# Marking every DMA of a batched matrix product as a single packet

## The chip, the cores and the metric

The kernel runs on one core of a Trainium2 chip. The time is the device time of one execution in microseconds. Every execution quoted with an interval was of the fast state; kernels with a single timing are of unknown state and are said to be single. A profile's span is some 2 us shorter than the device time (121.4 against 123.31 us for the kernel before); it runs from the start of the first instruction in the trace to the end of the last. Ratios are the mean time of one kernel's fast runs over the mean of the other's of the same rounds, so they are not quite the ratios of the medians quoted beside them.

## The reference

```python
batch, m, k, n = 16, 512, 512, 512
a: (batch, k, m) float32,  b: (batch, k, n) float32
return np.matmul(a.transpose(0, 2, 1), b).astype(np.float32)
```

The kernel reads 2 x 16.8 MB and writes 16.8 MB. Both inputs are cast to bfloat16 on the way to the matrix engine.

## The kernel before

Two batches ("a pair") stand in a tile of 128 partitions, 64 each. A partition holds 8 rows of 512 floats, which lie side by side in memory: one run of 16 KB. (With a size, a run is here such a stretch of bytes.) The first loads and the two halves of the last one have 4 rows, 8 KB. A store moves 8 KB from each partition for each batch. SP issues all 24 DMAs, on one queue. The profile lists 16 DMA engines. Shared evenly among them (an estimate: the trace's 1664 rows of 16 KB over 13 loads and 16 engines are 8 each), an engine moves 8 partitions of each DMA: 8 runs of a load, 32 runs of a store of four batches.

```python
in_v = [x.rearrange("(pair g) (q r) m -> pair (g q) r m", g=G, r=R) for x in (a, b)]
out_v = out.rearrange("batch (c t) n -> c batch t n", t=T)
# ...
for n in range(2, 2 * pairs):
    if n >= NX:                                  # NX = 4 input buffers
        nc.sync.wait_ge(s_in, n - NX + 1)        # free when DVE has cast the buffer
    src, x = in_v[n % 2][n // 2], x_ts[n % NX]
    if n < 2 * pairs - 1:
        nc.sync.dma_start(x[:], src).then_inc(s_x[n % NX], 16)
    # ... (the last load in two halves)
nc.sync.wait_ge(s_h, 16)                         # stores only after the loads
for i in range(0, NO, 2):
    n = min(2, NO - i)
    nc.sync.wait_ge(s_out, i + n)
    nc.sync.dma_start(out_v[:, G * i:G * (i + n)],
        o_t[:, i:i + n].rearrange("p i g t n -> p (i g) t n")).then_inc(s_o if i else s_o0, 16)
# ... casts on DVE, matmuls on PE, copies of PSUM on ACT
nc.sync.dma_start(out_v[:, batch - G:batch], o_ts[(pairs - 1) % NO])   # the last store
```

## Time and profile before

| | kernel before |
|---|---|
| device time, median | 123.31 us (123.14 to 123.31, 3 runs) |
| span of the profile | 121.4 us |
| PE, DVE, ACT busy | 51%, 31%, 27% |
| sixteen DMA engines | 97.7% |
| 2 MB load, issue to landing | 12.2 us (a), 15.9 us (b) |

A DMA is said to land with the last of its sixteen semaphore writes (the trace has 384 of them, records of 4 B, for 24 DMAs). The table reads as follows. A compute engine that is busy half of the time has room; the DMA engines have none. So the time is the number of bytes over the rate at which the engines move them (50.33 MB at the load window's 429 GB/s are 117.3 us), plus the two ends. The lines that carry this are shown in the prediction.

### The profile page before, as it was taken

How to read it: one execution, taken by the hardware profiler on the slowest of the kernel's cores; microseconds unless marked ns; L12 is line 12 of the kernel's file. 1: busy time of each engine (PE TensorE's matmuls, PEld its weight loads, DVE VectorE, ACT ScalarE, POOL GpSimd, SP SyncE). 2: the span in 40 equal slices, each digit the busy share in tenths (PEclk: the TensorE clock that was granted, in tenths of full speed). 3: DMA queues.
4: the chain of work that ended last, by engine and by line, in shares of the span. 5: the costliest groups of instructions: out<-in, count | busy, mean ns of one | idle time of the engine just before them, and what ended most of it. 6: DMA issues, size and time to landing. Idle time of an engine off the chain costs nothing.

```text
span 121.4 us, 1204 instructions
## 1 busy us (share of the span) xinstructions
PE 61.7 (51%) x480; PEld 35.0 (29%) x480; DVE 38.1 (31%) x48; ACT 32.2 (27%) x41; POOL 0.2 (0%) x4
## 2 busy tenths in 40 slices
PE   0007829099379559959919979989800000000000
PEld 0002314066156225536515636655400000000000
DVE  0061160864284090484265347492000000000000
ACT  4000423302900920390560084190009200000000
POOL 0000000000000000000000000000000000000000
PEclk9999999999999967999995999999995555555555
DMA  2999999999999999999999999999999999999994
GB/s 57 424 432 429 467 432 432 432 432 432 432 432 432 432 432 427 432 432 416 432 427 427 432 432 402 432 427 427 429 429 432 429 429 432 421 424 429 429 424 208
DMA packets 4864, 50.33 MB, mean 415 GB/s; under 512 B 384, under 2 KB 384, under 8 KB 384
## 3 DMA queue, kind: packets, MB, share of 16 engines
q1 hardware_dynamic: 4864, 50.33, 97.7%
HBM read 33.55 MB, written 16.78 MB: 415 GB/s over the span
## 4 chain that ended last, share of the span: by engine, by line
DMA 63%; DVE 6%; issue 3%; ACT 2%; SPq 2%; ACTq 1%
DMA x<-in_b_dram 53%; DMA out_dram<-o 10%; DVE bbf L118 3%; DVE abf L118 3%; ACT o L181 2%; SPq L74 1%; ACTq L70 1%; SPq L72 1%; SPq L80 0%; DVE done L124 0%; ACT done L186 0%; SPq L219 0%; SPq L70 0%
## 5 line engine op out<-in xcount | busy, mean ns | idle before, releaser
L156 PE MATMUL ps<-bbf,abf 64*128 64x512 bf16 x448 | 53.0, 393 | 13.6 <-PEq L151 13.6
L156 PEld LDWEIGHTS ps<-bbf,abf 64*128 64x128 bf16 x448 | 31.3, 112 | 35.3 <-issue 20.6
L181 ACT COPY o<-ps 128x1024 f32<-128x1024 f32 x28 | 26.3, 1026 | 45.9 <-PE ps L156 37.0
L118 DVE CAST abf<-x 128x2048 bf16<-128x2048 f32 x14 | 17.1, 1224 | 17.5 <-PE ps L156 13.5
L118 DVE CAST bbf<-x 128x2048 bf16<-128x2048 f32 x14 | 17.1, 1225 | 14.6 <-DMA x<-in_b_dram 14.6
L136 PE MATMUL ps<-bbf,abf 128*128 128x512 bf16 x32 | 8.7, 433 | 12.4 <-PEq L134 12.4
L136 PEld LDWEIGHTS ps<-bbf,abf 128*128 128x128 bf16 x32 | 3.7, 121 | 16.9 <-issue 14.8
L175 ACT COPY o<-ps 128x1024 f32<-128x1024 f32 x4 | 4.0, 1012 | 15.9 <-PE ps L136 15.9
L99 DVE CAST abf<-x 128x2048 bf16<-128x2048 f32 x2 | 2.5, 1228 | 11.2 <-DMA x<-in_a_dram 5.8
L99 DVE CAST bbf<-x 128x2048 bf16<-128x2048 f32 x2 | 2.5, 1225 | 1.2 <-DMA x<-in_b_dram 1.2
L186 ACT ACTIVATE done<-done 1x1 uint32<-1x1 uint32 x8 | 1.6, 197 | 0.0
L175 ACT ACT_TABLE_LOAD x1 | 1.3, 1283 | 0.9 <-SPq L70 0.9
L124 DVE MEMSET done<- 1x1 f32 x14 | 0.8, 59 | 0.0
L103 DVE MEMSET done<- 1x1 f32 x2 | 0.1, 59 | 0.0
L208 POOL MEMSET const-bfloat16-1.0<- 128x1 bf16 x1 | 0.1, 102 | 0.0
L208 POOL MEMSET const-uint8-127<- 128x1 uint8 x1 | 0.1, 102 | 0.0
L208 POOL MEMSET const-float32-0.0<- 128x1 f32 x1 | 0.1, 99 | 0.2 <-issue 0.2
L208 POOL MEMSET const-float32-1.0<- 128x1 f32 x1 | 0.1, 99 | 0.0
## 6 DMA issues: line engine op xcount, KB each, us to landing
x<-in_a_dram SPq DMA_DIRECT2D x7, 2048.0 KB, 12.2
x<-in_b_dram SPq DMA_DIRECT2D x6, 2048.0 KB, 15.9
out_dram<-o SPq DMA_DIRECT2D x3, 4096.0 KB, 21.7
x<-in_b_dram SPq DMA_DIRECT2D x4, 1024.0 KB, 12.1
out_dram<-o SPq DMA_DIRECT2D x2, 2048.0 KB, 29.3
x<-in_a_dram SPq DMA_DIRECT2D x2, 1024.0 KB, 6.8
```

Source lines behind the costliest of these rows:

```text
L70: with tc.tile_critical(no_gpsimd_drain=True):
L72: nc.sync.dma_start(x_ts[j][:, 0:RV, :], in0_v[j][0]).then_inc(s_f[j], 16)
L74: nc.sync.dma_start(x_ts[j][:, RV:R, :], in0_v[j][1]).then_inc(s_x[j], 16)
L99: nc.vector.tensor_copy(out=bf_ts[0][:], in_=x_ts[j][:, u * RV:(u + 1) * RV, :]).then_inc(s_cast, 1)
L118: nc.vector.tensor_copy(out=(bbf_ts if n % 2 else abf_ts)[v][:], in_=x_ts[n % NX][:, v * RV:(v + 1) * RV, :],).then_inc(s_cast, 1)
L124: nc.vector.memset(dve_done[:, n:n + 1], 0.0).then_inc(s_in, 1)
L136: mm = nc.tensor.matmul(ps_ts[0][h][:, t % 2, :], a_m[:, r, t], bbf_ts[0][:, r, :], start=(r == 0), stop=(r == RV - 1),)
L156: mm = nc.tensor.matmul(ps_ts[g][h][:, t % 2, :], a_m[:, t], bbf_ts[v][rows, r, :], start=(v == 0 and r == 0), stop=(v == V - 1 and r == R ...
L175: nc.scalar.copy(out=o_ts[0][:, g, 2 * h:2 * h + 2, :], in_=ps_ts[0][h][:]).then_inc(s_ev[h], 1)
L181: ev = nc.scalar.copy(out=o_ts[i % NO][:, g, 2 * h:2 * h + 2, :], in_=ps_ts[g][h][:])
L186: nc.scalar.memzero(act_done[:, i:i + 1]).then_inc(s_out, 1)
L208: nc = _bacc.Bacc("TRN2", target_bir_lowering=False, num_devices=1)
```

## The change

By its name, the flag `single_packet` asks that all runs which one DMA engine moves for a DMA form one packet. That reading is mine. In the kernel before, the trace has a record for each run (4480 data records for 4480 runs). The intent is to save whatever a packet costs at its boundary.

```diff
+    def dma(dst, src):
+        return nc.sync.dma_start(dst, src, single_packet=True)
...
-                nc.sync.dma_start(x[:], src).then_inc(s_x[n % NX], 16)
+                dma(x[:], src).then_inc(s_x[n % NX], 16)
...  (likewise the first loads, the last load's halves and all stores)
```

## The prediction

> **What bounds the kernel now.** I read the page first, at its busy table and its slices, then the DMA queue and the sizes of its packets, then the chain that ended last, and last the windows and the waits of the DMA queue's own engine.
>
> The page of the kernel before:
>
> ```profile
> PE 61.7 (51%) x480; PEld 35.0 (29%) x480; DVE 38.1 (31%) x48; ACT 32.2 (27%) x41; POOL 0.2 (0%) x4
> ...
> DMA  2999999999999999999999999999999999999994
> GB/s 57 424 432 429 467 432 432 432 432 432 432 432 432 432 432 427 432 432 416 432 427 427 432 432 402 432 427 427 429 429 432 429 429 432 421 424 429 429 424 208
> DMA packets 4864, 50.33 MB, mean 415 GB/s; under 512 B 384, under 2 KB 384, under 8 KB 384
> ...
> q1 hardware_dynamic: 4864, 50.33, 97.7%
> ...
> DMA 63%; DVE 6%; issue 3%; ACT 2%; SPq 2%; ACTq 1%
> ```
>
> No compute engine is busy much over half of the span, while the DMA row is at 9 (90% or more) in 38 of 40 slices, and the one data queue fills 97.7% of sixteen engines' time. The GB/s row is flat: there is no stage in which the DMA engines starve. So the kernel is bound by the DMA engines from 2 to 120 us, and the chain (63% DMA) says the same in another way. A compute saving would buy nothing; only a change of the time per byte, or of the two ends, can move the total.
>
> The windows, whose last two columns are the share of the DMA engines and their rate, put numbers on the stages (first loads in 8 KB rows, loads in 16 KB rows, stores in 8 KB rows):
>
> ```profile
> 2.00:12.70 10.70, 2.99 (x8) 1.09 (x9) 2.45 (x2) 0.18 (x1) 0.00 (x0) 1.00 1.01 413
> 12.70:76.00 63.30, 47.34 (x374) 27.13 (x374) 30.79 (x40) 23.24 (x30) 0.00 (x0) 0.95 1.00 429
> ...
> 80.80:120.10 39.30, 6.87 (x64) 4.04 (x59) 1.72 (x4) 5.23 (x8) 0.00 (x0) 0.63 1.00 424
> ```
>
> The reader is to see that the share stays at 1.00 in the load stage and in the store stage, with the store stage about 1% slower.
>
> The waits of the issuing engine, SP, tell whether the queue ever runs dry:
>
> ```profile
> SPq L80 <- DVE done L124: 43.8, 9, 8.3
> SPq L219 <- DMA out_dram<-o: 24.9, 1, 24.9
> ...
> x<-in_b_dram SPq DMA_DIRECT2D x6, 2048.0 KB, 15.9
> out_dram<-o SPq DMA_DIRECT2D x3, 4096.0 KB, 21.7
> ```
>
> SP waits for free buffers, but a 2 MB load takes 15.9 us from issue to landing, and at 432 GB/s its own transfer is 2.097 MB / 432 = 4.9 us. So some three loads stand in the queue at any time, and what it costs to issue or to start one is hidden behind the others. At the end SP waits 24.9 us for the last store: the tail is pure queue, too.
>
> **What the trace's DMA records add.** Taken one by one, the records of the data queue are of three sizes: 1664 of 16384 B that take 611 ns each, 2816 of 8192 B that take 309 ns, and 384 of 4 B that take 9 ns. The first two are the contiguous rows, one per partition (8 rows of 512 floats on a load; 4 rows on the first loads, on the last load's halves and on the stores); 384 = 24 DMAs x 16 engines are the semaphore writes. Per engine: 104 x 0.611 = 63.5, 176 x 0.309 = 54.4 and 24 x 0.009 = 0.2, together **118.1 us**; the first record starts at 1.97 us and the last ends at 120.07 us, which is also 118.1 us. The records tile the time of each engine without a hole. And two 8 KB records take 618 ns where one 16 KB record takes 611: so a record costs **7 ns plus 302 ns for each 8 KB**. The 7 ns is the only thing per run that a coarser packet could remove. 302 ns for 8192 B on 16 engines is 434 GB/s.
>
> [...]
>
> **The change part by part.** The order of instructions on each engine, compared between the two programs, is unchanged: 24 DMAs on SP, same shapes, same waits; the diff only adds a flag.
> - Removed: packet boundaries between the rows of one DMA on one engine. There are 104 + 176 = 280 data rows per engine in 24 DMAs, so 280 - 24 = 256 boundaries go. If the whole 7 ns is paid per packet, that is 256 x 7 = 1.79 us. [...] If the 7 ns belongs to the descriptor, it is 0. All of it lies on the path that sets the end, since the engines are never idle: whatever goes there shows in full.
> - Added: at most 0.4 us at the first load, where nothing hides it. [...] The semaphore writes remain: 24 per engine, 0.2 us.
> - Moved: the landing of each load, and with it DVE's casts, PE and the buffers' release, come earlier or later with the stream; PE has 49% of the span free, so it stays hidden. ACT's 8.9 us wait for the first store ends with that store; the last store is issued at 95.0 us, while its records begin only at 115.2, so there are 20 us of slack.
>
> The sum with a weight of 0.5 on the full 7 ns, 0.3 on half of it, 0.2 on nothing: 0.9 + 0.27 = 1.17 us off, minus some 0.1 for the start: about **1.1 us off 123.31, so 122.2 us**.
>
> **The rivals.**
> - *Nothing happens.* The 7 ns belong to each descriptor [...], or the records keep 611 and 309 ns: 123.3 us. [...] Against it: a fixed cost of 7 ns a record is plainly there.
> - *The long packet hurts.* An engine might [...] make a bubble at each of the 24 boundaries [...]. For it: [...] one store issue of SP took 5.5 us against 0.69 in the median[...]. [...] A bubble of 0.1 us at each of 24 boundaries gives +2.4 us, 124.6 us after the gain; one of 0.2 us gives over 126.
> - *The bound moves elsewhere.* With DMA 1.5% faster, would PE or DVE take over? PE 61.7 and DVE 38.1 us of 121.4 say no.
>
> **Range and chances.** The best case is 123.31 - 1.79 = 121.5 us, 1.5% off: even the full sum does not reach 2%. So faster by over 2% (under 120.8 us) would need a saving that I cannot see: 0.05. Slower by over 2% (over 125.8 us) is the second rival with bubbles of 0.17 us or more: 0.10. Within 2%: 0.85. The range of 8 in 10 runs from 121.3 (the best case with a little of the launch's spread, 0.17 us in the three runs) to 124.0 us (no gain and a small bubble).
>
> **What would show each step right or wrong.** Right: the number of DMA records falls from 4864 towards 24 x 16 of data plus 384, or it stays while a row takes 302 to 306 ns in place of 309 and 604 to 608 in place of 611; GB/s in load slices goes from 432 to 433 or 434, and the store window from 424 to 428 or more; the span goes down by 1 us or so with the DMA share still near 97.7%. Wrong towards the first rival: 611 and 309 unchanged. Wrong towards the second: zeros or sevens in the DMA row where there are nines, a GB/s row that dips at DMA boundaries, or records longer than 309 ns in the store stage. The start: the first landing, now at 5.8 us, should not come over 0.4 us later. [...]

Passages that rest on nothing these traces show are cut from the prediction, and the cuts are marked. The forecast's sum: 0.5 x 1.79 + 0.3 x 0.90 + 0.2 x 0 = 1.17 us off, and 1.1 us off after 0.1 us for the start. The 0.90 us is half of the 1.79 us, and that half of the 7 ns might be saved was not shown. The 0 to 0.4 us at the start was an estimate from the first issue, which took 0.39 us in the trace. "Descriptor" stands for a single run, whether it is joined with others or not.

## The result, and the profile after

The changed kernel took 123.17 us in the median (123.11 to 123.35, 4 runs) against 123.25 us of the kernel before in the same rounds (123.14 to 123.31). The ratio is 0.9997, with a 95% interval of 0.998 to 1.0014: no change. All outputs are right.

The page of the kernel after, its DMA rows, the count of packets and the data queue:

```profile
DMA  2999999999999999999999999999999999999994
GB/s 54 426 426 431 474 431 431 431 431 431 431 431 431 431 431 431 431 431 431 431 431 431 431 431 388 428 431 423 428 423 426 431 428 431 431 423 431 426 428 175
DMA packets 4864, 50.33 MB, mean 414 GB/s; under 512 B 384, under 2 KB 384, under 8 KB 384
...
q1 hardware_dynamic: 4864, 50.33, 97.6%
```

The count is the first thing to see: 4864 packets, as before. (What the page counts as packets are the records of the trace: each has a start, a length and a size.) If runs had been joined, and a record stood for a packet, 4480 data records would have become 384. The DMA row and the share (97.6% and 97.7%) are the same. The rates are the same too, which the windows show (columns: window and its length, busy time of PE, its weight load, DVE, ACT and POOL, the granted clock, the share of the DMA engines, GB/s). The kernel after:

```profile
12.70:76.00 63.30, 49.00 (x364) 26.97 (x364) 30.79 (x40) 23.24 (x30) 0.00 (x0) 0.93 1.00 430
...
80.80:120.10 39.30, 8.21 (x74) 4.75 (x70) 2.37 (x4) 6.92 (x10) 0.00 (x0) 0.67 1.00 425
```

Before, these two windows had 429 and 424 GB/s. Record by record, all 1664 rows of 16 KB take 611 ns in both traces, and of the 2816 rows of 8 KB all but some sixty take 309 ns in both. In steady state two 2 MB loads land 4862 ns apart in both traces, in the mean of twelve. Small differences elsewhere, such as PE's 64.9 us busy after against 61.7 before, lie on engines with idle time: the change did not touch their instructions, and PE's granted clock dips at other moments (its mean in the load window is 0.95 before and 0.93 after).

So nothing happened, to the nanosecond of a record. That is more than "the saving was small": even a flag that made one boundary cheaper by 1 ns would have moved the landings of 2 MB loads, with their 7 inner boundaries on each engine, by 7 ns. The question became whether the flag acts at all.

**What the built programs say.** Both kernels were compiled and the results compared. In the program handed to the compiler all 24 DMAs carry the flag, false before and true after. In the output, the instruction streams of all five engines are byte for byte the same; only the tables that map instructions to source lines differ, beside logs and the compiler's copy of its input. No run's page shows this; flag_off below has these same streams too. So the theory that I took to the chip: **the compiler drops the flag, and the chip runs the same program twice.** The rival: the flag acts by some other way, and does nothing visible at rows of 8 and 16 KB, where a boundary weighs little (by my reading, 7 of 309 and of 611 ns).

### The profile page after: what moved, and what is told of

The parts are those of the page before. It is cut to its first block, busy times and chain, and to the rows that moved or that the text cites. A ratio compares the mean times of both kernels' runs of the same rounds, so it can differ in the third digit from the quotient of the medians.

```text
span 121.6 us, 1204 instructions
## 1 busy us (share of the span) xinstructions
PE 64.9 (53%) x480; PEld 35.7 (29%) x480; DVE 38.0 (31%) x48; ACT 32.2 (26%) x41; POOL 0.2 (0%) x4
## 2 busy tenths in 40 slices
DMA packets 4864, 50.33 MB, mean 414 GB/s; under 512 B 384, under 2 KB 384, under 8 KB 384
## 3 DMA queue, kind: packets, MB, share of 16 engines
q1 hardware_dynamic: 4864, 50.33, 97.6%
HBM read 33.55 MB, written 16.78 MB: 414 GB/s over the span
## 4 chain that ended last, share of the span: by engine, by line
DMA 45%; DVE 7%; PE 4%; issue 3%; ACT 2%; ACTq 1%
DMA x<-in_b_dram 35%; DMA out_dram<-o 10%; PE ps L140 4%; DVE abf L122 4%; DVE bbf L122 3%; ACT o L185 2%; ACTq L74 1%; DVE done L128 0%; ACT done L190 0%
## 5 line engine op out<-in xcount | busy, mean ns | idle before, releaser
L140 PE MATMUL ps<-bbf,abf 128*128 128x512 bf16 x32 | 11.8, 552 | 12.5 <-PEq L138 12.5
L140 PEld LDWEIGHTS ps<-bbf,abf 128*128 128x128 bf16 x32 | 4.3, 139 | 19.6 <-issue 19.0
```

The source lines that it names most:

```text
L140: mm = nc.tensor.matmul(ps_ts[0][h][:, t % 2, :], a_m[:, r, t], bbf_ts[0][:, r, :], start=(r == 0), stop=(r == RV - 1),)
```

## The experiments

**The same program twice, and the noise.** flag_off is the changed kernel with

```diff
-        return nc.sync.dma_start(dst, src, single_packet=True)
+        return nc.sync.dma_start(dst, src, single_packet=False)
```

and flag_on is the changed kernel again, both five rounds on one chip.

> The changed kernel with the flag set to False: the kernel before under another name, for the noise of the method. Every theory: ratio 1.000 to the kernel before, with an interval of about 0.2% to each side.

> The changed kernel again, on the same chip as flag_off. Theory (the compiled instruction streams of the two programs came out byte for byte the same, so the flag does nothing on the chip): ratio 1.000, as flag_off within 0.1%, rows of 611 and 309 ns as before. Rival (the flag acts, and a small gain hides in the noise of the first four runs): 0.2 to 0.5 us under flag_off, or some rows under 611 ns.

| | median us | ratio to before | 95% interval |
|---|---|---|---|
| flag_off | 123.09 | 0.9992 | 0.9978 to 1.0006 |
| flag_on | 123.20 | 0.9997 | 0.9983 to 1.001 |

The kernel before under another name differs from itself by 0.08%, and the flag from that by 0.05%, in the wrong direction for a saving. A gain of 1.1 us would be 0.9%, far outside either interval. flag_on's rival (a gain of 0.2 us or more, hidden in noise) has no support left: flag_on came out 0.11 us above flag_off.

**Short runs, where a packet's cost would weigh.** The loads are cut into runs of 2 KB, without and with the flag; data and buffers stay the same, and the stores keep their 8 KB:

```diff
+    def load(dst, src):
+        return nc.sync.dma_start(dst, src, single_packet=False, max_dma_last_dim=2048)
...
-                dma(x[:], src).then_inc(s_x[n % NX], 16)
+                load(x[:], src).then_inc(s_x[n % NX], 16)
```

> Loads cut into runs of 2 KB (64 runs per engine for 2 MB), flag off. Theory (7 ns of fixed cost per run, on the path): a record of 2048 B takes 302/4 + 7 = 82 to 83 ns; per engine 1024 x 82.5 = 84.5 us of loads in place of 78.4, so 6 us more: 129.3 us. If the 7 ns is not a cost per run (but grows with the bytes): 77 ns and 123.3 us.

> As rows2k_off, with the flag on. Theory (the flag is dropped): 129.3 us and records of 82 to 83 ns, ratio to rows2k_off 1.000. Rival (the flag acts, but buys nothing at rows of 8 KB and more): the packets are joined, records of 76 to 79 ns, 122 to 126 us, 3 to 7 us under rows2k_off.

Measured: 127.39 us without the flag and 127.38 with it (ratios to before 1.0334 and 1.0337, intervals of 0.16% to each side). Here are the rates in the load stage, first the kernel before, then rows2k_off, then rows2k_on:

```profile
20.00:75.00 55.00, 41.74 (x346) 24.19 (x345) 28.42 (x36) 20.63 (x28) 0.00 (x0) 0.94 1.00 430
```

```profile
20.00:75.00 55.00, 43.14 (x335) 25.07 (x333) 24.81 (x31) 18.78 (x25) 0.00 (x0) 0.91 1.05 409
```

```profile
20.00:75.00 55.00, 42.22 (x334) 23.64 (x332) 24.82 (x31) 19.07 (x25) 0.00 (x0) 0.92 1.05 409
```

The rate fell from 430 to 409 GB/s, and the flag gave nothing back. But my expectation of 129.3 us missed by 2 us, and the line says why: the share of the DMA engines is 1.05. Records cover more time than there is, so they **overlap**, and the length of a record is not what it costs. A 2 KB record takes 84 ns, but two 2 MB loads of 64 runs per engine landed 5126 ns apart. Less some 8 ns for the semaphore write (an estimate: its record is 9 ns), that is 80.0 ns a run. The same reading of the kernel before gives 606.8 ns for a 16 KB run (not 611) and, from two stores landing 9794 ns apart with 32 runs, 305.8 ns for 8 KB (not 309). These three fit **37.64 ns for each KB and 4.7 ns for each run** within 0.2 ns. My 7 ns came from the lengths of records. With 4.7 the expectation would have been 1024 x 80.0 = 81.9 us in place of 104 x 606.8 + 48 x 305.8 = 77.8 us of loads: 4.1 us more, and 4.2 were measured.

**512 B.** The same edit with 512 in place of 2048 puts this to a test.

> Loads cut into runs of 512 B, flag off. From the spacing of the semaphore writes the rows of 16, 8 and 2 KB fit 37.6 ns per KB plus 4.7 ns per run; so a run of 512 B should take 23.5 ns, the loads of one engine 4096 x 23.5 = 96.3 us in place of 77.8: 18.5 us more, about 141.7 us. If 7 ns per run were right after all: 25.9 ns, 151 us. Longer still if SP cannot make the descriptors fast enough; then the DMA row shows holes.

> As rows512_off with the flag on: here a fixed cost per packet would weigh most. Theory (the flag is dropped): as rows512_off within 0.3%. Rival (the flag acts where rows are short): down by up to 18 us.

Measured: 141.74 us without the flag, 141.73 with it (ratios 1.15 and 1.1505). The fit foretold 141.7. The load stage of rows512_off and rows512_on:

```profile
20.00:75.00 55.00, 41.12 (x272) 20.98 (x272) 20.18 (x25) 15.10 (x20) 0.00 (x0) 0.81 1.15 348
```

```profile
20.00:75.00 55.00, 37.61 (x271) 19.72 (x269) 20.17 (x25) 16.30 (x22) 0.00 (x0) 0.89 1.15 348
```

512 B on 16 engines at 348 GB/s is 16 x 512 / 348 = 23.5 ns a run, while the records say 27 ns, with a share of 1.15. In this kernel of 65536 load runs the fixed cost adds 18.5 us to that of the kernel before, all on the path, and the flag still takes off nothing.

One rival to this reading is that SP, and not the DMA engines, sets the pace here. SP's issues of these loads take 5.96 us in the median, nearly as long as the 6.03 us between two landings:

```profile
L74 SPq DMA_DIRECT2D x<-in_b_dram x10: 1906/5963/6189, 1.4 to 90.8; - x10
```

(columns behind the count: shortest, median and longest issue in ns). The expectation named the sign of it, holes in the DMA row. There are none: 38 of the 40 slices are at 9, and the records of 27 ns still overlap, by 3.5 ns, where those of 2 KB (84 ns in 80.0) and 16 KB (611 in 606.8) overlap by 4. And the fit that foretold 23.5 ns rests on longer runs, at which SP had time to spare: in the kernel before an issue took 0.33 us of 4.86. So the cost is laid to the DMA engines; no run of its own tested it.

From SP the flag does nothing at any length tried. The built programs say so too: the instruction streams of rows2k_off and rows2k_on are byte for byte the same, and so are those of rows512_off and rows512_on. The times of each pair differ by noise alone; what the pairs measure is the cost of a run.

**Would joined packets have helped?** That is the other half of my prediction, and the flag cannot answer it. But GpSimd's DMAs are on a queue of another kind: the profile lists it as software_dynamic and SP's as hardware_dynamic. To see whether runs are joined there, rows2k_off was changed so that GpSimd issues the loads and waits for free buffers, with separate semaphores for the stores:

```diff
-        return nc.sync.dma_start(dst, src, single_packet=False, max_dma_last_dim=2048)
+        return nc.gpsimd.dma_start(dst, src, single_packet=False, max_dma_last_dim=2048)
```

> The loads in runs of 2 KB, flag off, issued from GpSimd in place of SP[...]. If it joins them and the fixed cost is one of packets: semaphore writes of two 2 MB loads 4.83 us apart in place of 5.13 (75 ns a run). If it does not join them, or the cost is one of runs: 5.13 us (80 ns a run)[...].

> The loads in rows of 16 KB, as in the kernel before, issued from GpSimd: the control for pool2k_off. Expected: 2 MB loads 4.86 us apart as from SP (607 ns a row), the whole at 123 to 126 us[...].

Measured, a single timing each: 126.59 us for 2 KB runs and 124.04 us for 16 KB rows. The count of packets and the GpSimd queue of pool2k_off:

```profile
DMA packets 10624, 50.33 MB, mean 403 GB/s; under 512 B 384, under 2 KB 384, under 8 KB 8576
## 3 DMA queue, kind: packets, MB, share of 16 engines
q0 software_dynamic: 8496, 33.56, 66.1%
```

GpSimd did join runs: 33.55 MB in 2 KB runs are 16384, but the queue has 8496 records, which are 8192 of 4096 B and 304 semaphore writes. Two runs of 2 KB stand in one record. Loads landed 5012 ns apart, or 156.4 ns a packet of two runs, where two lone runs from SP take 2 x 79.97 = 159.9 ns: one boundary less saves 3.5 ns. The 4.83 us that I expected of joined runs left out that a packet of two still has one boundary; with it the sum is 32 x (150.6 + 4.7) + 8 ns = 4.98 us. The control with 16 KB rows, which it leaves alone (one row a record), costs 606.8 ns a row, exactly as from SP; its 0.8 us over the kernel before (123.22 us in those rounds) matches the start, where the first load landed 0.8 us later (6.6 us against 5.8).

**More runs to a packet.** rows4k_off is the SP kernel with 4096 in place of 2048, a lone run in a packet of 4096 B. pool1k_off, pool512_off and pool512_on are the GpSimd kernel with 1024 and 512, the last with the flag.

> Loads cut into runs of 4 KB from SP: packets of 4096 B with one run each, the control for GpSimd's packets of two. At 37.6 ns per KB plus 4.7 ns per packet of one run: 155.3 ns, two 2 MB loads 4.98 us apart, the whole 1.7 us over the kernel before, 124.9 us.

> Runs of 1 KB from GpSimd. pool2k_off showed records of 4096 B (two runs joined) at 156.4 ns; if the 4.7 ns of a lone run are 3.5 ns per packet and 1.2 ns per run, a packet of four runs takes 150.6 + 3.5 + 4 x 1.2 = 158.9 ns and two 2 MB loads lie 5.09 us apart. If everything were per packet (and pool2k_off's extra 1 ns something else): 155 to 157 ns, 4.98 to 5.02 us. If everything were per run: 169 ns, 5.43 us.

> Runs of 512 B from GpSimd, flag off: eight to a packet of 4096 B if it joins them. By 3.5 ns per packet and 1.2 ns per run: 150.6 + 3.5 + 8 x 1.2 = 163.5 ns, two 2 MB loads 5.24 us apart (from SP they were 6.03), the whole about 129 us in place of SP's 141.7. All per packet: 155 to 157 ns, 5.0 us. All per run: 188 ns, 6.03 us. Holes in the DMA row if GpSimd cannot make 4096 runs per load in that time.

> As pool512_off with the flag on. Theory (the flag is dropped on GpSimd's path too; the compiled streams are the same): packets of 4096 B as before, same spacing. Rival (the flag widens GpSimd's packets): records larger than 4096 B, fewer of them.

Measured, a single timing each: 125.05, 129.07, 135.31 and 135.39 us. Again the load stages, in the order rows4k_off, pool2k_off, pool1k_off, pool512_off, pool512_on:

```profile
20.00:75.00 55.00, 41.88 (x332) 23.22 (x332) 26.89 (x33) 21.11 (x28) 0.00 (x0) 0.91 1.02 422
```

```profile
20.00:75.00 55.00, 42.22 (x333) 23.23 (x331) 25.36 (x32) 20.76 (x27) 11.65 (x12) 0.91 1.02 418
```

```profile
20.00:75.00 55.00, 41.02 (x335) 23.69 (x333) 24.91 (x31) 18.90 (x25) 15.77 (x12) 0.94 1.02 406
```

```profile
20.00:75.00 55.00, 37.25 (x290) 20.68 (x292) 25.01 (x31) 17.38 (x23) 20.38 (x11) 0.91 1.02 384
```

```profile
20.00:75.00 55.00, 38.19 (x284) 21.05 (x286) 25.35 (x34) 17.78 (x24) 21.54 (x11) 0.89 1.02 384
```

All five have packets of 4096 B, and DMA engines without holes in this stage, so the last column gives the cost of a packet, for pool512_off 16 x 4096 / 384 = 171 ns. With the landings for exactness:

| runs in a packet of 4096 B | ns a packet | over 150.6 ns for the bytes | lone runs would take | saved per boundary removed |
|---|---|---|---|---|
| 1 (SP, rows4k_off) | 155.2 | 4.6 | | |
| 2 (pool2k_off) | 156.4 | 5.8 | 159.9 | 3.5 |
| 4 (pool1k_off) | 161.1 | 10.5 | 169.4 (from the fit) | 2.8 |
| 8 (pool512_off, _on) | 170.5 | 19.9 | 188.2 | 2.5 |

rows4k_off came out as expected (155.3 ns, and 125.05 us against 124.9). pool1k_off and pool512_off did not (expected 158.9 and 163.5 ns, and about 129 us for pool512_off): I had split the 4.7 ns into 3.5 per packet (what pool2k_off had saved) and 1.2 per run, which holds for two runs only; with four and eight, a run inside a packet keeps about 2.4 ns. That the whole cost is per run (188 ns) and that it is all per packet (155 to 157 ns) are both ruled out on this path: joining four or eight saves somewhat over half of the 4.7 ns for each boundary removed (2.8 and 2.5 ns). At 512 B the kernel took 135.3 us with GpSimd's joined runs (a single timing) against 141.7 us with SP's lone ones. And the flag did nothing on this path either: same packets, same 384 GB/s, 0.08 us apart, and the same compiled streams.

The last column sets GpSimd's joined runs against SP's lone ones. At 16 KB a lone row costs the same from both (606.8 ns), which speaks against a cost of the path itself, but lone short runs from GpSimd were not measured.

What stays open: the figures for joined packets are GpSimd's, with up to eight runs in 4 KB. Packets of 8 or 32 whole rows from SP never came about, so whether they would save 2.5 ns a boundary, or lose something of another kind, no run shows. Why the compiler drops the flag wasn't looked for either.

## Why the prediction was wrong

**The bound, the queue and the path: right.** The kernel is bound by the DMA engines, and whatever a run costs shows in full in the total. The kernels with 2 KB and 512 B runs show it best: the fixed costs there put 4.2 and 18.5 us on the total, what the fit gives for the engines alone. Compute stayed hidden throughout: PE, the busiest of the compute engines, was busy for 48% to 53% of the span in every profile.

**The step that failed is "Removed: packet boundaries between the rows of one DMA on one engine".** The prediction saw that the order of instructions was the same on each engine and that "the diff only adds a flag", and then went on as if the flag were an instruction to the DMA engines. It gave 0.8 to some saving, and 1.1 us to the mean. In fact no boundary went: 4864 records before and after, landings 4862 ns apart before and after, and compiled streams that are the same. The prediction had a rival by which nothing happens, at 0.2 and 123.3 us, which is what came. But its reason (the 7 ns belong to each descriptor, so that joining saves nothing) was not the cause, so that its number is right by luck. The fault lay one layer up, where I did not look: comparing the built programs would have settled it before any run.

**The 7 ns were mis-sized.** "A record costs 7 ns plus 302 ns for each 8 KB" measured 4.7 ns and 301 ns: records overlap, by 3 to 4 ns each. The check that I drew comfort from, 118.1 us of records in 118.1 us of time, closed by chance. At the measured cost an engine's work is 104 x 606.8 + 176 x 305.8 ns and 0.2 us of semaphore writes, 117.1 us. The missing 1.0 us lies at the ends: the first load kept the engines for 3.3 us in the mean, where later ones of its size land 2.45 us apart (the records of the first 5 us are stretched, 361 ns in the mean in place of 309), and the engines end up to 0.4 us apart. So the best case was not 256 x 7 = 1.79 us but 256 x 4.7 = 1.2 us; and with the 2.5 to 3.5 ns that a removed boundary saved on GpSimd's path, an estimate for a flag that works is 256 x 2.5 to 256 x 3.5 = **0.6 to 0.9 us**, 0.5 to 0.7%. My weights had led to 1.17 us.

**The added cost at the start (0 to 0.4 us) and the rival of the long packet that hurts: not tested**, since no long packet was ever made. The chances (0.85 within 2%) and the range held the result; the centre forecast a gain that the flag could not give.

## What to carry to other kernels

Before estimating what a flag is worth, find out whether it reaches the machine: compare the compiled streams, or look at a count that it must change (here, the packets of the page). Take the cost of a DMA run from the distance between landings of queued transfers or from the rate in a stage, not from the length of its record: here records overlapped, 27 ns of record for every 23.5 ns of time at 512 B. Where the engines are full, as here (97.7%), long runs are the lever: 4.7 ns a run is 0.8% of a 16 KB run (606.8 ns) and a fifth of a 512 B run (23.5 ns), and the loads ran at 430, 409 and 348 GB/s in runs of 16 KB, 2 KB and 512 B.
